# Norm weights at the split, weight work behind the norm chain, one more kept unit, and a skip term on TensorE, in a two-layer trunk kernel

## The chip, the cores and the metric

The kernel runs on one core of a Trainium2 chip. The metric is the device time of one execution in microseconds (us), lower is better. Three timed runs of the kernel before took 2191.85, 2193.81 and 2197.32 us; their median is 2193.81 us. A separate, profiled execution gives the trace.

The engines are named as in the profile: PE is TensorE's matmul, PEld its weight load, DVE is VectorE, ACT is ScalarE, POOL is GpSimd, and SP issues the DMAs from one queue, in order.

## The reference, cut to what matters

One sequence of 256 tokens, width 2048, goes through two layers. Layer 0 mixes with a diagonal state-space model (S5) and a gated linear unit (GLU), layer 1 with latent attention. Each is followed by a gated feed-forward part (FFN) with a short causal convolution. Around every part stand two RMS norms with their own weights: one on what the part puts out, one on what the next part reads.

```python
for l in range(DEPTH):                      # 2 layers
    h = rmsnorm(x, norm_g[l, 0])
    m = s5_mixer(h, ...) if l == 0 else mla_mixer(h, ..., *shared_kv(x, kv_norm_g, ...))
    x = x + rmsnorm(m, norm_g[l, 1])        # weight gpost
    h = rmsnorm(x, norm_g[l, 2])            # weight gpre of the FFN
    f = conv_ffn(h, ...)                    # (gelu(conv(h @ w_gate)) * (h @ w_up)) @ w_down
    x = x + rmsnorm(f, norm_g[l, 3])
# rmsnorm(x, g) = x * rsqrt(mean(x*x) + 1e-6) * g
# in s5_mixer: y = einsum(h_re, c_re) - einsum(h_im, c_im) + d_skip * u
```

All of it is float32. `d_skip * u` is the skip term.

## The kernel before, in words

**Split products.** A float32 product is made of three matmuls (`mm3`, L108 to L110) on a high and a low part of each operand. `split` (L73, L74) makes the parts: ScalarE copies the source into a rounded high part, VectorE subtracts that from the source. `wunit` (L77) loads a unit of weights, 1 MB, into one of two buffers called `raw` and splits it in two halves; each half costs one ScalarE and one VectorE instruction on 128x1024. The parts go into rotating buffers (`whi`, `wlo`, three each) or, with `slots=`, into places of their own where they can stay (tiles named `x` in the profile).

**Tokens in two blocks.** The 256 tokens are two blocks of 128 (`tb` 0 and 1). Activations for the next part are kept transposed and split, in four tiles `act`.

**Stages.** S5 in 16 rounds of 8 channel groups (on all engines, with early GLU units put in between), the rest of the GLU, FFN of layer 0, attention, FFN of layer 1. In the FFN, 21 of the 22 pairs of weight columns use activations of both blocks as the moving operand (`inner`, L114 and L115).

**The turn between two parts** is what the change is about; there are three: GLU to FFN, FFN to attention, attention to FFN. Each goes like this.

1. The last weight units of a part are *kept* (`held`): block 0 is multiplied as each arrives (5 units in the GLU by `HOLD5` and `LATE`, 4 in attention's output projection by `HOLD`), and the matmuls of block 1 on the same units come after that. They are TensorE's work while block 0 goes through its norms.
2. `finish_chunk` (L163 to L166) takes the sum of squares of each 512 columns on ScalarE (L139) and multiplies by `gpost` on VectorE (L166). In the GLU, `finish` (L629 to L632) comes before it: two bias additions, a sigmoid on ScalarE, a product.
3. `post_norm` (L168): `rstd1` (L141 to L153) adds the sums (`tot`, L145), GpSimd takes a power (`rs_y`, L147), three tiny VectorE instructions refine it (L149, L151, L153). Then for each of the four chunks, L172 adds the normed output to `x`, ScalarE takes the squares of the new `x` (L139), and, where the next part is an FFN, L178 multiplies `x` by `gpre` into `f`.
4. `pre_scale` (L180): a second `rstd1`, and L182 scales the identity matrix by it. Call the instruction d0 for block 0 and d1 for block 1.
5. `pre_turn` (L185 to L192): 16 matmuls (32 records in the profile) with d0 or d1 as the moving operand transpose and scale a block at once (L191); each bank of four is split into `act`.
6. The next part's first weight units are kept too: four units, multiplied for block 0 (`swapped`, L708, in the FFN; `down` in attention), then block 1's `pre_turn` (that is `tail()`), then block 1's products.

So d0 is what TensorE waits for after the kept units, and d1 is what it waits for after block 0's products on the next four.

**What sets the order.** Each engine works through its instructions in one fixed order. A scheduler makes that order when the program is built, by priority and by a model of when operands are ready. It therefore puts splits of the next part's weights between the steps of the norm chain wherever the model has them ready.

**S5.** `part_k` sums products of small tiles in PSUM (`tiled`, L399), ScalarE copies 112 of 128 columns of each group into `K` (L451), VectorE adds the skip term `dB` to the last 16 while copying them (L452), and 128 records of small matmuls read `K` (L467).

**Other loads.** `gkv` and `gq` are the first DMAs of the program (L604, L605), ahead of S5's own; the `gpre` and `gpost` rows are broadcast to all partitions, 1 MB each (`gain_load`, L134).

Of the kernel before, what the change touches and what calls it, by code (L numbers as in the profile page):

```python
# [35 lines left out]
HOLD5 = ((0, 2), (4, 6), (10, 12), (8, None), (None, None))  # L36
LATE = ((1, 1), (2, 1), (3, 1), (2, 0), (3, 0))
# [7 lines left out]
def tile_trunk(ctx: ExitStack, tc: tile.TileContext, a: dict):  # L45
# [84 lines left out]
    def gain_tile(src):  # L130
        return T(env["ap"], [P, D], F32, "gb", 2), src
# [31 lines left out]
    def finish_chunk(f, fst, tb, n, g):  # L163
        c = f[tb][:, n * 512 : (n + 1) * 512]
        sq_acc(c, fst[tb][:, n : n + 1])
        dve.tensor_tensor(c, c, g[0][:, n * 512 : (n + 1) * 512], op=ALU.mult)  # L166

    def post_norm(f, fst, tb, x, xst, g):  # L168
        r = rstd1(fst[tb], D)
        for n in range(NCH):  # L170
# [6 lines left out]
            if g is not None:  # L177
                dve.tensor_tensor(f[tb][:, c], x[tb][:, c], g[0][:, c], op=ALU.mult)  # L178

    def pre_scale(xst):  # L180
        d = T(env["ap"], [P, 512], F32, "xh", 2)[:, :P]
        dve.tensor_scalar(d, ident, rstd1(xst, D), None, op0=ALU.mult)  # L182
        return d

    def pre_turn(h, d, tb):  # L185
        for n in range(NCH):
# [5 lines left out]
            split(*acts4(tb, n, slice(0, 4)), ptv)  # L192
# [50 lines left out]
    def glu_early(f, n, b, half):  # L243
        hv = glu_load(n, b, half)
        banks = [accb(), accb()]
        for tb in range(NB):
            hk, u = hv
            for i, (wh, wl) in enumerate(u):
                for k in range(hk):
                    j = i * hk + k  # L250
                    mm3(banks[tb], *acts(tb, 4 * b + j), wh[:, k, :], wl[:, k, :], j == 0, j == 3)
        o = half * 1024 + n * 512
# [8 lines left out]
    def s5(f):  # L261
        with tc.tile_pool(name="s5", bufs=2) as q1:
            w0 = env["wp"]
            dt = T(q1, [P, P], F32, "dt", 1)
            sync.dma_start(dt, a["sL"].partition_broadcast(P))
            sA = T(q1, [P, 2, P], F32, "sA", 1)
            sync.dma_start(sA, a["sA"])
            sync.dma_start(cst, a["cst"])
# [6 lines left out]
            sync.dma_start(dB, a["dX"])  # L275

# [117 lines left out]
            def tiled(*terms):  # L394
                o = wk()[:, : NG * P]
                for g in range(NG):
                    for i, (lhs, rhs) in enumerate(terms):
                        for j in range(4):
                            pe.matmul(  # L399
                                o[32 * j : 32 * j + 32, g * P : (g + 1) * P], lhs(g, j), rhs(g, j),  # L400
                                start=g == 0 and i == 0, stop=g == NG - 1 and i == len(terms) - 1,
                                tile_position=(0, 32 * j),
                            )
                return o
# [33 lines left out]
            def part_k(sb, e1, ff):  # L438
# [7 lines left out]
                def e67(g, j):  # L446
                    return flat2(e1[:, 4 * g + j, 6:8, :])

                pkg = by_group(tiled(*((e67, lambda g, j, z=z: flat2(z[:, 4 * g + j, 1:9, :])) for z in ff)))
                K = Ks[sb % 2]  # L450
                act.activation(K[:, :, :112], pkg[:, :, :112], AF.Copy)  # L451
                dve.tensor_tensor(  # L452
                    K[:, :, 112:128],
                    pkg[:, :, 112:128],
                    dB.rearrange("p (g q) -> p g q", q=16)[:, NG * sb : NG * (sb + 1), :],
                    op=ALU.add,
                )
# [360 lines left out]
    def attention(tail, gains, f, fst, done):  # L818
        with tc.tile_pool(name="at", bufs=2) as q1:
# [200 lines left out]
            for g in gains:  # L1020
                gain_load(g)
# [157 lines left out]
```

## Time and profile before

| what | us |
|---|---|
| timed runs, median (lowest to highest) | 2193.81 (2191.85 to 2197.32) |
| the profiled execution | 2187.58 |
| its span, first to last instruction | 2185.8 |
| PE busy in the span | 2079.0 (95%) |
| VectorE busy | 1408.8 (64%) |
| ScalarE busy | 1122.4 (51%) |
| GpSimd busy | 19.8 (1%) |

The profiled execution is one run; the 1.78 us between its time and its span lie around the first and the last instruction. Rows of a timeline read: start, duration, engine, line of the kernel, operation, out<-in with the shapes, count, and in brackets how long the engine had stood still before it and what ended that. Rows of the table of windows read: window, its length, then for PE, PEld, DVE, ACT and POOL the busy us and in brackets the instructions, then TensorE's granted clock as a share of full speed, the DMA engines' busy share, and GB/s. A busy time of an instruction includes some overlap with its neighbour: instructions that follow each other directly start a little sooner than the durations say.

### The profile page before, as it was taken

How to read it: one execution, taken by the hardware profiler on the slowest of the kernel's cores; microseconds unless marked ns; L12 is line 12 of the kernel's file. 1: busy time of each engine (PE TensorE's matmuls, PEld its weight loads, DVE VectorE, ACT ScalarE, POOL GpSimd, SP SyncE). 2: the span in 40 equal slices, each digit the busy share in tenths (PEclk: the TensorE clock that was granted, in tenths of full speed). 3: DMA queues.
4: the chain of work that ended last, by engine and by line, in shares of the span. 5: the costliest groups of instructions: out<-in, count | busy, mean ns of one | idle time of the engine just before them, and what ended most of it. 6: DMA issues, size and time to landing. Idle time of an engine off the chain costs nothing.

```text
span 2185.8 us, 32404 instructions
## 1 busy us (share of the span) xinstructions
PE 2079.0 (95%) x13268; PEld 1764.2 (81%) x13268; DVE 1408.8 (64%) x1940; ACT 1122.4 (51%) x1695; POOL 19.8 (1%) x57
## 2 busy tenths in 40 slices
PE   3788999899999999999989999989999999999998
PEld 2566777888888888888878998788888888888886
DVE  7999666666466556655686665566646655665567
ACT  6677445455455445544464554545545544554444
POOL 0000000000000000000000000000000000000000
PEclk9999999999999999999999999999999999999999
DMA  4132476455565555555564434635555555555654
GB/s 131 50 98 75 154 233 206 145 188 179 193 197 187 193 193 191 178 190 193 192 200 129 136 118 155 212 123 189 189 193 193 180 187 193 193 183 184 194 191 154
DMA packets 280966, 374.74 MB, mean 171 GB/s; under 512 B 9200, under 2 KB 196208, under 8 KB 279792
## 3 DMA queue, kind: packets, MB, share of 16 engines
q1 hardware_dynamic: 280816, 372.66, 52.4%
q8 instruction: 104, 1.70, 0.3%
q14 instruction: 46, 0.38, 0.1%
HBM read 370.54 MB, written 2.10 MB: 170 GB/s over the span
## 4 chain that ended last, share of the span: by engine, by line
PE 82%; DVE 10%; DMA 4%; ACT 3%; issue 1%; POOL 0%; SPq 0%; DVEq 0%; POOLq 0%; ACTq 0%
PE wk L114 29%; PE wk L115 15%; PE acc L108 9%; PE acc L109 9%; PE acc L110 9%; DMA raw<-in_w_glu 3%; PE wk L108 2%; PE wk L109 2%; PE wk L110 2%; DVE wlo L74 2%; PE acc L191 1%; DVE x L74 1%; ACT whi L73 1%; DVE f L431 1%; DVE f L430 1%
## 5 line engine op out<-in xcount | busy, mean ns | idle before, releaser
L74 DVE TENSOR_TENSOR wlo<-raw,whi 128x1024 fp32r<-128x1024 f32 (+2 forms) x640 | 761.0, 1191 | 584.0 <-ACT whi L73 579.3
L73 ACT ACTIVATE whi<-raw 128x1024 fp32r<-128x1024 f32 (+2 forms) x640 | 658.3, 1031 | 635.3 <-PE wk L114 245.6
L114 PE MATMUL wk<-act,whi 128*128 128x512 f32 x2688 | 941.9, 395 | 0.0
L115 PE MATMUL wk<-act,wlo 128*128 128x256 f32 x2688 | 753.0, 280 | 0.0
L114 PEld LDWEIGHTS wk<-act,whi 128*128 128x128 f32 x2688 | 504.1, 188 | 119.3
L115 PEld LDWEIGHTS wk<-act,wlo 128*128 128x128 f32 x2688 | 507.4, 189 | 0.3
L108 PE MATMUL acc<-whi,hh 128*128 128x512 f32 x652 | 255.4, 392 | 0.0
L109 PE MATMUL acc<-wlo,hh 128*128 128x512 f32 x652 | 255.3, 392 | 0.0
L110 PE MATMUL acc<-whi,hl 128*128 128x512 f32 x652 | 254.3, 391 | 0.0
L108 PEld LDWEIGHTS acc<-whi,hh 128*128 128x128 f32 x652 | 122.4, 188 | 27.2 <-ACT hh L73 0.5
L109 PEld LDWEIGHTS acc<-wlo,hh 128*128 128x128 f32 x652 | 122.4, 188 | 27.0 <-DVE wlo L74 0.5
L110 PEld LDWEIGHTS acc<-whi,hl 128*128 128x128 f32 x652 | 122.4, 188 | 26.9
L108 PE MATMUL acc<-whi,act 128*128 128x512 f32 (+1 forms) x332 | 126.4, 381 | 2.7 <-ACT act L73 2.7
L109 PE MATMUL acc<-wlo,act 128*128 128x512 f32 (+1 forms) x332 | 124.9, 377 | 1.9 <-DVE wlo L74 1.9
L110 PE MATMUL acc<-whi,act 128*128 128x512 f32 (+1 forms) x332 | 124.3, 375 | 0.1
L765 DVE SCALAR_TENSOR_TENSOR cv<-gs,cw,cv 128x255 f32<-128x255 f32 (+1 forms) x168 | 77.2, 480 | 3.0
L109 PEld LDWEIGHTS acc<-wlo,act 128*128 128x128 f32 x332 | 62.5, 188 | 14.9 <-DVE wlo L74 4.0
L108 PEld LDWEIGHTS acc<-whi,act 128*128 128x128 f32 x332 | 62.5, 188 | 14.5 <-ACT act L73 3.0
L110 PEld LDWEIGHTS acc<-whi,act 128*128 128x128 f32 x332 | 62.5, 188 | 11.5 <-DVE act L74 0.5
L763 ACT ACTIVATE cv<-gs,cb,cw 128x256 f32<-128x256 f32 x84 | 50.5, 601 | 36.5 <-DVE gs L715 36.5
L714 ACT ACTIVATE us<-wk 128x256 f32<-128x256 f32 x84 | 31.7, 380 | 60.3 <-PE wk L115 60.3
L714 ACT ACTIVATE gs<-wk 128x256 f32<-128x256 f32 x84 | 32.0, 381 | 59.8 <-PE wk L115 59.8
(282 smaller groups left out, 2342.5 us busy)
## 6 DMA issues: line engine op xcount, KB each, us to landing
raw<-in_w_gate SPq DMA_DIRECT2D x88, 1024.0 KB, 5.0
raw<-in_w_up SPq DMA_DIRECT2D x88, 1024.0 KB, 4.9
raw<-in_w_down SPq DMA_DIRECT2D x88, 1024.0 KB, 4.9
raw<-in_w_glu SPq DMA_DIRECT2D x32, 1024.0 KB, 6.2
raw<-in_w_o SPq DMA_DIRECT2D x16, 1024.0 KB, 4.9
raw<-in_w_ukv SPq DMA_DIRECT2D x8, 1024.0 KB, 5.3
gb<-in_norm_g SPq DMA_DIRECT2D x6, 1024.0 KB, 6.7
raw<-in_w_uq SPq DMA_DIRECT2D x8, 768.0 KB, 4.4
```

The lines of the kernel that those rows point to most:

```text
L73: act.activation(hi, src, AF.Copy)
L74: (eng or dve).tensor_tensor(lo, src, hi.bitcast(F32), op=ALU.subtract)
L108: pe.matmul(o, lh, rh, start=first, stop=False)
L109: pe.matmul(o, lh, rl, start=False, stop=False)
L110: pe.matmul(o, ll, rh, start=False, stop=last)
L114: pe.matmul(ov, lh, r, start=first, stop=False)
L115: pe.matmul(ov[:, 0, :], ll, r[:, 0, :], start=False, stop=last)
L191: pe.matmul(ptv[:, k, :], h[:, o : o + P], d, start=True, stop=True)
L430: dve.tensor_tensor(f1, zt(0, 0, 9, 1), bc(2, 9), op=ALU.mult)
L714: act.activation(z[:, ft, :], two[ft][:, S:], AF.Copy)
L763: act.activation(cv[:, ft, :], gv[:, ft, :], AF.Identity, scale=cw[:, 2, n : n + 1], bias=cb[:, n : n + 1])
L765: dve.scalar_tensor_tensor(cv[:, ft, sh:], gv[:, ft, : S - sh], cw[:, 2 - sh, n : n + 1], cv[:, ft, sh:], op0=ALU.mult, op1=ALU.add,)
```

## The change

Five edits are made together.

- **Norm weights at the split.** `gpre` is no longer multiplied into `f` (L178 goes, with the 1 MB broadcast of the weights). It is loaded as a column per 128 channels (`gf`), and `pre_turn` applies it while splitting: per bank four ScalarE and four VectorE instructions on 128x128 with a scale pointer, where one of each on 128x512 stood.
- **Weight work behind the norm chain.** d0 is remembered (`env["turn"]`). `tc.issue_after(d0)` orders the VectorE instructions of a block of code behind d0 on VectorE. It is put around the splits of the next part's kept units (in the FFN all but the first, in attention the third and fourth), around block 1's `finish` in the GLU, and around block 1's `gpost` product elsewhere. It orders no instruction of another engine.
- **One more kept unit.** Six instead of five in the GLU; in the output projection the last unit of the third chunk of columns is kept as well, and block 1's part of that chunk moves behind block 0's end. One `gb` buffer goes.
- **Skip term on TensorE.** Four small matmuls with the identity (columns of 32) add `dB` to the PSUM bank; ScalarE copies all 128 columns, and L452 goes.
- **Order of the first loads.** `sA` comes first, then `dt`; `gkv`, `gq` and the new `gf` come behind S5's loads.

```diff
-HOLD5 = ((0, 2), (4, 6), (10, 12), (8, None), (None, None))
-LATE = ((1, 1), (2, 1), (3, 1), (2, 0), (3, 0))
+HOLD6 = ((0, 2), (4, 6), (10, 12), (14, 16), (8, None), (None, None))
+LATE = ((1, 1), (2, 1), (3, 1), (1, 0), (2, 0), (3, 0))
...
-        return T(env["ap"], [P, D], F32, "gb", 2), src
+        return T(env["ap"], [P, D], F32, "gb", 1), src
...
     def finish_chunk(f, fst, tb, n, g):
         c = f[tb][:, n * 512 : (n + 1) * 512]
         sq_acc(c, fst[tb][:, n : n + 1])
-        dve.tensor_tensor(c, c, g[0][:, n * 512 : (n + 1) * 512], op=ALU.mult)
+        with behind(env["turn"] if tb else None):
+            dve.tensor_tensor(c, c, g[0][:, n * 512 : (n + 1) * 512], op=ALU.mult)
...
             sq_acc(x[tb][:, c], xst[:, n : n + 1])
-            if g is not None:
-                dve.tensor_tensor(f[tb][:, c], x[tb][:, c], g[0][:, c], op=ALU.mult)
...
+    def behind(ins):
+        return nullcontext() if ins is None else tc.issue_after(ins)
+
-            split(*acts4(tb, n, slice(0, 4)), ptv)
+            hi, lo = acts4(tb, n, slice(0, 4))
+            if g is None:
+                split(hi, lo, ptv)
+                continue
+            for k in range(4):
+                gk = g[:, 4 * n + k : 4 * n + k + 1]
+                act.activation(hi[:, k, :], ptv[:, k, :], AF.Copy, scale=gk)
+                dve.scalar_tensor_tensor(
+                    lo[:, k, :], ptv[:, k, :], gk, hi[:, k, :].bitcast(F32), op0=ALU.mult, op1=ALU.subtract
+                )
...
-            sync.dma_start(dt, a["sL"].partition_broadcast(P))
             sA = T(q1, [P, 2, P], F32, "sA", 1)
             sync.dma_start(sA, a["sA"])
+            sync.dma_start(dt, a["sL"].partition_broadcast(P))
...
+            for z, v in ((gkv, a["gkv"]), (gq, a["gq"]), (gf[0], a["gf"][0]), (gf[1], a["gf"][1])):
+                sync.dma_start(z, v)
...
+                if diag is not None:
+                    for j in range(4):
+                        pe.matmul(
+                            by_group(o)[32 * j : 32 * j + 32, :, 112:128], ident[:, 32 * j : 32 * j + 32], diag,
+                            start=False, stop=True, tile_position=(0, 32 * j),
+                        )
...
-                act.activation(K[:, :, :112], pkg[:, :, :112], AF.Copy)
-                dve.tensor_tensor(
-                    K[:, :, 112:128],
-                    pkg[:, :, 112:128],
-                    dB.rearrange("p (g q) -> p g q", q=16)[:, NG * sb : NG * (sb + 1), :],
-                    op=ALU.add,
-                )
+                act.activation(K[:, :, :P], pkg, AF.Copy)
...
-                    if n == 3 and (b, half) > (1, 0):
+                    if n == 3 and (b, half) > (0, 1):
...
-                    gain_load(gains[1])
...
-            finish(3, tb, banks, bb)
+            with behind(env["turn"] if tb else None):
+                finish(3, tb, banks, bb)
...
-                                held.append((which, kh, wunit(v, 8, S, slots=HOLD[len(held)])))
+                                with behind(before if held else None):
+                                    held.append((which, kh, wunit(v, 8, S, slots=HOLD[len(held)])))
...
+                    with behind(before if which == 0 and un > 1 else None):
+                        hv = wunit(
...
-                    if n < NCH - 1:
+                    if n == NCH - 2 and un == 3:
+                        late = (load(n, un, (10, 12)), banks)
+                        down(banks[0], un, 0, late[0])
+                        chunk(n, 0, banks)
+                    elif n < NCH - 1:
                         project(n, un, banks)
...
-                for tb in range(NB):
-                    if tb:
+                for tb in range(NB if n == NCH - 2 else 0, NB):
+                    if tb and held:
+                        down(late[1][1], 3, 1, late[0])
+                        chunk(NCH - 2, 1, late[1])
                         for un, hv in enumerate(held):
                             down(banks[1], un, 1, hv)
...
-                    dg[tb] = pre_scale(xst[tb])
+                    dg[tb], ins = pre_scale(xst[tb])
+                    if tb == 0:
+                        env["turn"] = ins
             elif not last:
-                pre_turn((x if gn is None else f)[tb], dg[tb], tb)
+                pre_turn(x[tb], dg[tb], tb, gpre)
```

More of the change, by code (lines that the diff above doesn't have):

```diff
@@ L1 @@
 import math
-from contextlib import ExitStack
+from contextlib import ExitStack, nullcontext
 import concourse.bass as bass
@@ L251, in glu_early, with glu_keep @@
                     mm3(banks[tb], *acts(tb, 4 * b + j), wh[:, k, :], wl[:, k, :], j == 0, j == 3)
+        glu_keep(f, n, b, half, banks)
+    def glu_keep(f, n, b, half, banks):
         o = half * 1024 + n * 512
@@ L603, in tile_trunk @@
     gkv, gq = T(cp, [P, KT], F32, "gkv"), T(cp, [P, KT], F32, "gq")
-    sync.dma_start(gkv, a["gkv"])
-    sync.dma_start(gq, a["gq"])
+    gf = [T(cp, [P, KT], F32, f"gf{l}") for l in range(2)]
     krE, krO = T(cp, [P, S], F32, "krE"), T(cp, [P, S], F32, "krO")
@@ L622, in rope_tables, with glu_rest @@
         sincos(rsin, rcos, rr, rn, cst[:, C_RS : C_RS + 1])
-    def glu_rest(q1, todo, f, fst, gains, done):
+    def glu_rest(q1, todo, f, fst, gain, done):
         def finish(n, tb, banks, bb):
@@ L632, in finish @@
             dve.tensor_tensor(c, c, sg, op=ALU.mult)
-            finish_chunk(f, fst, tb, n, gains[0])
+            finish_chunk(f, fst, tb, n, gain)
         def bias(n):
@@ L660, in glu_rest @@
                     if b == 0:
-                        gain_load(gains[0])
+                        gain_load(gain)
                     bb = bias(b)
@@ L678, in glu_rest, with ffn @@
                 done(0, 1)
-            finish(3, tb, banks, bb)
+            with behind(env["turn"] if tb else None):
+                finish(3, tb, banks, bb)
             done(tb, 0)
         return lambda: done(1, 1)
-    def ffn(l, tail, gains, f, fst, done):
+    def ffn(l, tail, before, gain, f, fst, done):
         with tc.tile_pool(name=f"ff{l}", bufs=2) as q1:
@@ L775, in ffn @@
                 if part == len(PARTS) - 2:
-                    for g in gains:
-                        if g is not None:
-                            gain_load(g)
+                    gain_load(gain)
                 def load(n, un, slots=(None, None)):
@@ L790, in evac @@
                     if last:
-                        finish_chunk(f, fst, tb, n, gains[0])
+                        finish_chunk(f, fst, tb, n, gain)
                 if last:
@@ L815, in ffn, with attention @@
         return lambda: done(1, 1)
-    def attention(tail, gains, f, fst, done):
+    def attention(tail, before, gpost, f, fst, done):
         with tc.tile_pool(name="at", bufs=2) as q1:
@@ L1018, in attention, with chunk @@
                     q = {"kv": kv, "qn": qn, "qr": rope(q1, qs_, br[:, S:])}
-            for g in gains:
-                gain_load(g)
+            gain_load(gpost)
+            env["yp"] = q1
+            def chunk(n, tb, banks):
+                c = f[tb][:, n * 512 : (n + 1) * 512]
+                act.activation(c, banks[tb], AF.Copy)
+                finish_chunk(f, fst, tb, n, gpost)
             for n in range(NCH):
@@ L1030, in attention @@
                         down(banks[0], un, 0, held[un])
-                for tb in range(NB):
-                    if tb:
+                for tb in range(NB if n == NCH - 2 else 0, NB):
+                    if tb and held:
+                        down(late[1][1], 3, 1, late[0])
+                        chunk(NCH - 2, 1, late[1])
                         for un, hv in enumerate(held):
                             down(banks[1], un, 1, hv)
-                        if held:
-                            done(0, 1)
-                    c = f[tb][:, n * 512 : (n + 1) * 512]
-                    act.activation(c, banks[tb], AF.Copy)
-                    finish_chunk(f, fst, tb, n, gains[0])
+                        done(0, 1)
+                    chunk(n, tb, banks)
                     if held:
@@ L1146, in _arrays @@
         "b_glu": g("ssm_b_glu"),
+        "gf": np.stack([pn(g("norm_g")[l, 2]) for l in range(2)]),
         "gkv": pn(g("kv_norm_g")),
```

43 lines of the change are left out of this document (23 added, 20 removed).

## The prediction, made before the changed kernel was run

> **What bounds the kernel now.** I read the page first, then the table of windows, then the timelines of single engines around the places where TensorE stands still.
>
> ```profile
> span 2185.8 us, 32404 instructions
> PE 2079.0 (95%) x13268; PEld 1764.2 (81%) x13268; DVE 1408.8 (64%) x1940; ACT 1122.4 (51%) x1695; POOL 19.8 (1%) x57
> ...
> 50.00:200.00 150.00, 123.21 (x2157) 91.54 (x2142) 144.09 (x234) 104.69 (x208) 0.43 (x6) 0.99 0.25 73
> 340.00:372.00 32.00, 30.90 (x129) 23.52 (x128) 18.42 (x18) 16.16 (x20) 0.00 (x0) 1.00 0.69 204
> 1460.00:2165.00 705.00, 704.99 (x3716) 602.53 (x3715) 426.02 (x500) 346.89 (x441) 0.00 (x0) 1.00 0.57 188
> ```
>
> The last row is the second FFN: TensorE never stops, and nothing in the change touches its matmuls. The kernel can win only in the 107 us in which TensorE is idle: in S5, where VectorE is the bound (144.09 of 150), in the GLU, and at the turns. TensorE's timeline shows the three turns, and a warm `pre_turn` to compare with:
>
> ```profile
> 393.24 6.28 PE L191 MATMUL acc<-xh,f 128*128 128x128 f32 x32 [7.29 <-DVE xh L182]
> 410.76 3.73 PE L191 MATMUL acc<-xh,f 128*128 128x128 f32 x32
> 1145.34 5.72 PE L191 MATMUL acc<-xh,x 128*128 128x128 f32 x32 [5.92 <-DVE xh L182]
> 1428.87 5.61 PE L191 MATMUL acc<-xh,f 128*128 128x128 f32 x32 [7.41 <-DVE xh L182]
> ...
> 389.00:390.00 1.00, 0.00 (x0) 0.00 (x0) 1.00 (x3) 1.00 (x2) 0.67 (x1) 0.50 0.00 0
> 301.00:302.00 1.00, 1.00 (x3) 0.75 (x3) 0.16 (x1) 0.00 (x0) 0.00 (x0) 0.50 0.82 215
> ```
>
> At each turn TensorE waits 5.9 to 7.4 us for d0 (L182), and the 32 records after it take 5.6 to 6.3 us where the warm ones take 3.73: in the stall the granted clock falls to 0.50. The two FFN turns thus cost at most 7.29 + 2.55 and 7.41 + 1.88, 19.1 us together.
>
> **What the change does to the first turn.** VectorE's timeline from block 0's last bias (L631) to d0, and to d1, with the windows and groups of that stretch:
>
> ```profile
> 375.60 0.69 DVE L631 TENSOR_TENSOR f<-acc,bias 128x512 f32<-128x512 f32 x1 [1.75 <-PE acc L110]
> 380.18 1.23 DVE L74 TENSOR_TENSOR x<-raw,x 128x1024 fp32r<-128x1024 f32 x1 [0.22 <-ACT x L73]
> 392.30 0.69 DVE L166 TENSOR_TENSOR f<-f,gb 128x512 f32<-128x512 f32 x1
> 392.90 0.28 DVE L182 TENSOR_SCALAR xh<-cst,rs_r 128x128 f32<-128x128 f32 x1
> 405.39 0.29 DVE L182 TENSOR_SCALAR xh<-cst,rs_r 128x128 f32<-128x128 f32 x1
> ...
> 375.60:393.18 17.58, 10.35 (x45) 8.07 (x43) 17.29 (x32) 11.97 (x21) 2.04 (x3) 0.86 0.54 178
> 393.18:405.68 12.50, 12.44 (x86) 12.44 (x87) 11.31 (x24) 4.95 (x12) 2.08 (x4) 0.79 0.78 264
> ...
> L74 DVE TENSOR_TENSOR x<-raw,x 128x1024 fp32r<-128x1024 f32 x5 | 6.0, 1220 | 0.2 <-ACT x L73 0.2
> L74 DVE TENSOR_TENSOR wlo<-raw,whi 128x1024 fp32r<-128x1024 f32 x3 | 3.6, 1219 | 0.0
> L178 DVE TENSOR_TENSOR f<-x,gb 128x512 f32<-128x512 f32 x8 | 5.2, 685 | 0.0
> ```
>
> VectorE is full, 17.29 of 17.58 us, before d0. Eight weight splits stand in the two windows. Four of them, of the second and third kept unit, stand ahead of d0, the one at 380.18 the first, and will be ordered behind it: 4 x 1.14 (durations less the overlap of about 0.08) = 4.6 us. Block 1's four `finish` instructions (one like 392.30 each) go behind it: 4 x 0.6 = 2.4. The four L178 of block 0 vanish: 2.4. That is 9.4 us, and leaves 7.9 us of work. But the full engine hid the chain's other waits: two GpSimd powers, and the last ScalarE squares behind the last L172.
>
> ```profile
> 380.04 0.55 POOL L147 TENSOR_TENSOR rs_y<-tot,cst 128x1 f32<-128x1 f32 x1 [273.01 <-DVE tot L145]
> 389.33 1.45 POOL L147 TENSOR_TENSOR rs_y<-tot,cst 128x1 f32<-128x1 f32 x1 [8.70 <-DVE tot L145]
> ```
>
> I put these at 3.5 us: two powers near 0.55 to 1.45 plus hand-overs, and about 1.3 us for the last squares, with one ScalarE weight copy of the third unit still in between, since only VectorE is ordered. So d0 starts at 375.6 + 7.9 + 3.5 = 387.0, 5.9 us earlier. The kept matmuls end at 393.24 - 7.29 = 385.95. The sixth unit adds 12 matmuls of 30.90/129 = 0.24 us behind block 0's end, 2.9 us at most; but TensorE is already 97% busy there (row 340 to 372), so most of this is work only moved among itself, and I count 1 us. The gap left is 0.3 us (0 to 2).
>
> [...]
>
> **What is late next: d1.** Behind d0 now stand the six splits of units two to four, block 1's finish and norm chain, and block 0's splits with the weight in them. The nearest rows for the short instructions are of S5:
>
> ```profile
> 21.29 2.45 ACT L347 ACTIVATE act<-raw,rs_r 128x128 f32<-128x128 f32 x8
> 8.07 0.29 DVE L220 SCALAR_TENSOR_TENSOR R<-w,e 128x128 f32<-128x128 f32 x1
> ```
>
> On VectorE four times 0.25 (0.29 less overlap, plus a little for the pointer) replace 0.6 per bank: +1.6 us per block. On ScalarE four times 2.45/8 = 0.31 replace 0.5: +2.9 us per block, beside `pre_turn` and the first `swapped` products, which need a further bank only every 1.4 us (a bank serves half a unit, an eighth of the 11.3 us from 399.5 to 410.76): I cost it at nothing; without that cover it is 0.7 us for the first bank. VectorE's whole work from L631 to d1 changes by -4.8 (eight L178) + 1.6, and gains the 3.5 us of exposed waits: d1 stays near 405.4 + 0.3 = 405.7. Before, d1 had 5 us to spare, as TensorE came to block 1's `pre_turn` only at 410.76. Now TensorE would come there at 387.3 + 3.7 + 11.3 = 402.3 and wait for d1. So the turn gains 410.8 - 405.7 = 5.1 us, not 9.8. Ends: 8.5 if the splits fill the chain's holes well and d1 is in time; 2 if the fourth unit is late, whose load cannot be issued until the second unit's split frees its `raw` buffer, now behind d0; SP's later loads queue behind that one, and the first FFN products wait for it.
>
> **The third turn** is the same without `finish`:
>
> ```profile
> 1422.88 2.35 DVE L74 TENSOR_TENSOR x<-raw,x 128x1024 fp32r<-128x1024 f32 x2
> 1428.53 0.28 DVE L182 TENSOR_SCALAR xh<-cst,rs_r 128x128 f32<-128x128 f32 x1
> 1439.63 0.29 DVE L182 TENSOR_SCALAR xh<-cst,rs_r 128x128 f32<-128x128 f32 x1
> ...
> 1415.90:1428.81 12.91, 5.57 (x25) 4.22 (x23) 12.27 (x26) 7.67 (x15) 3.34 (x5) 0.88 0.48 158
> 1428.81:1439.92 11.11, 11.05 (x80) 11.05 (x81) 10.90 (x22) 6.39 (x14) 1.51 (x4) 0.83 0.59 220
> ```
>
> Ahead of d0 go four splits (two at 1422.88), four L178 and one L166: 7.6 of 12.3 us; with 3.5 us exposed d0 comes at 1424.1, 4.4 us earlier. TensorE ran dry at 1421.46; with 1 us of cover the gap is 1.7 us. The row at 301 us, behind gaps of 0.86 and 0.76 us, shows that even this can halve the clock for about 3 us, so I add 0.8. `pre_turn` then ends at 1428.6 and block 0's products at 1439.9. d1: 1439.6 - 4.8 + 1.6 + 0.6 (the moved chunk's L166) + 3.0 = 1440.0. So 1440.3 against 1445.75: 5.4 us (2 to 8.5). [...]
>
> **The second turn** loses only block 1's products with `gpost` ahead of d0; its third and fourth unit stand behind d0 already.
>
> ```profile
> L166 DVE TENSOR_TENSOR f<-f,gb 128x512 f32<-128x512 f32 x2 | 1.4, 688 | 0.1
> ```
>
> Two such between 1143.5 and d0: 1.2 us less, gap 4.7. I take 1.0 (0 to 1.2).
>
> **S5, start and GLU.**
>
> ```profile
> L452 DVE TENSOR_TENSOR K<-wk,dB 128x32 f32<-128x32 f32 x16 | 2.9, 182 | 2.5 <-ACT K L451 2.5
> 32.66 1.94 PE L399 MATMUL wk<-f,e 128*32 128x128 f32 x32 [8.18 <-DVE e L435]
> ...
> 0.74 0.38 SPq L604 DMA_DIRECT2D gkv<-in_gkv  x1
> 2.11 0.43 SPq L267 DMA_DIRECT2D sA<-in_sA  x1
> 5.50 0.43 DVE L300 TENSOR_TENSOR pu<-sA 128x256 f32<-128x256 f32 x1 [5.50 <-DMA sA<-in_sA]
> ...
> 285.85 0.50 SPq L134 DMA_DIRECT2D gb<-in_norm_g  x1
> 298.88 0.50 PE L109 MATMUL wk<-wlo,act 128*128 128x512 f32 x1 [0.76 <-DVE wlo L74]
> ```
>
> L452 frees VectorE of 16 x 0.12 and of 2.5 us of waiting, 4.4 us at best. In its place come eight matmul records a round, at 1.94/32 = 0.06 each 0.5 us, or 7.8 us in 16 rounds if all lay on the path; TensorE has 27 us of room in the 150. I take +1.0 (-5 to +4.4). At the start VectorE waits for `sA`, which moves to the head of the queue, 1.37 us earlier; `dt` and the inputs gain 0.9: 1.0 (0.5 to 1.4). The four small loads now queue ahead of the rounds' own; at 0.4 us an issue they delay those by some 0.8 us net, which S5's range covers. The broadcast at 285.85 goes: 1 MB less where the loads set the pace, just before two gaps and the halved clock at 301: 1.5 (0 to 3).
>
> Sum: 5.1 + 5.4 + 1.0 + 1.0 + 1.0 + 1.5 = 15.0 us. The profiled execution, 2187.58, would go to 2172.6. It lies 6.2 us below the median of the runs; against the median I forecast 2193.8 - 15.0 = 2178.8 us.
>
> **Rivals.**
> - *d1 is in time.* VectorE's holes are filled, and both FFN turns give 8.5; with the ends of the rest (1.2, 4.4, 1.4, 3) the gain is 27: 2167. For: VectorE is idle 3.5 us longer in the chain and could split there if the scheduler's order allowed it; against: the edges forbid just that.
> - *The wait moves.* The fourth unit's load or the first splits stall `swapped`, or ScalarE's unordered weight copies hold the squares back, or the scheduler put other VectorE work into the opening: the turns give 2 each, the rest 2: gain 6, 2188. For: SP stands in order behind the `raw` buffer; against: 8.5 us pass before the fourth unit is used.
> - *Slower: the identity matmuls do not overlap.* If each of the eight records runs alone for about 0.28 us, a round gets 2.2 us longer between ScalarE's copy and L467, 36 us in all; less 14 elsewhere and 4.4 on VectorE that makes 2211. It decides from 1.6 us a round. Against: the same column tiles run at 0.06 in the row at 32.66, and TensorE has room.
> - *The edges bind nothing* (the order was nearly so already): then the L178 and the loads alone remain, about 7: 2187. The row at 380.18 speaks against it.
>
> **How the numbers follow.** Forecast 0.56, d1 in time 0.13, the wait moves 0.18, slower 0.06, edges bind nothing 0.07. A measurement of this kernel can tell about 0.3%, 6.6 us. Faster by more than that are the first two (0.69), a third of the moved wait (0.06) and under half of the last (0.03): 0.78; slower is the identity matmuls' 0.06; the rest, 0.16, is the same. The range runs from the first rival, 2167, to the second, 2188, and some 3 us beyond each for the spread of the runs: 2164 to 2191.
>
> **What would show it.** Right: no L178, no L452; d0 some 6 and 4 us earlier after block 0's end, gaps before L191 under 2.5 us at the FFN turns, its 32 records near 3.7 us, and TensorE waiting for d1 before block 1's `pre_turn`. Wrong: gaps of 5 us at L191, a wait in `swapped` for L74 of the fourth unit, or longer rounds in S5.

## The result, and the profile after

The changed kernel took 2181.03 us (median of 4 runs, 2179.92 to 2182.69) against 2194.05 us for the kernel before (4 runs, 2191.85 to 2197.32): ratio 0.9942, 95% interval 0.9928 to 0.9956. A second measurement, among the experiments below, gave 2184.90 against 2193.22 us, ratio 0.9962 (0.9950 to 0.9974). So the change is worth 8 to 13 us; 15.0 were predicted, and 2178.8 us in a range of 2164 to 2191. The profiled execution took 2181.60 us, 6 us less than that of before, which was an unusually quick one.

The page, two lines:

```profile
span 2179.8 us, 32719 instructions
PE 2084.0 (96%) x13396; PEld 1765.9 (81%) x13396; DVE 1405.5 (64%) x1956; ACT 1135.1 (52%) x1743; POOL 18.5 (1%) x57
```

TensorE's timeline at the three turns (`pre_turn` is now L193; L108 is the first product of `swapped`):

```profile
388.20 3.84 PE L193 MATMUL acc<-xh,x 128*128 128x128 f32 x32
394.09 0.39 PE L108 MATMUL acc<-x,act 128*128 128x256 f32 x1 [2.05 <-DVE act L201]
407.22 3.84 PE L193 MATMUL acc<-xh,x 128*128 128x128 f32 x32 [1.46 <-DVE xh L181]
...
1142.69 5.87 PE L193 MATMUL acc<-xh,x 128*128 128x128 f32 x32 [4.77 <-DVE xh L181]
...
1419.46 3.84 PE L193 MATMUL acc<-xh,x 128*128 128x128 f32 x32 [0.91 <-DVE xh L181]
1424.83 0.38 PE L108 MATMUL acc<-x,act 128*128 128x256 f32 x1 [1.53 <-DVE act L201]
1438.31 3.84 PE L193 MATMUL acc<-xh,x 128*128 128x128 f32 x32 [1.77 <-DVE xh L181]
```

The long waits for d0 at the FFN turns are gone, and with them the half clock behind them: 3.84 us for the 32 records at a granted clock of 1.00, where 6.28 and 5.61 stood at a mean of 0.59 and 0.67. Two new waits are there at each FFN turn in this trace: one for short splits of `act` (L201) before `swapped` can start, which I call the gap at the first bank, and one for d1 before block 1's `pre_turn`. The name is short for more than it says: in both traces of this kernel, and at both FFN turns, TensorE goes on about 0.05 us after the end of the seventh of the sixteen short splits, though a bank has four. Why it is the seventh isn't shown. VectorE's timeline, with d0 and d1 (L181), and GpSimd's:

```profile
377.38 0.69 DVE L650 TENSOR_TENSOR f<-acc,bias 128x512 f32<-128x512 f32 x1 [1.75 <-PE acc L110]
386.59 0.16 DVE L145 TENSOR_REDUCE tot<-st 128x1 f32<-128x5 f32 x1 [1.13 <-ACT junk L139]
387.86 0.29 DVE L181 TENSOR_SCALAR xh<-cst,rs_r 128x128 f32<-128x128 f32 x1
406.88 0.29 DVE L181 TENSOR_SCALAR xh<-cst,rs_r 128x128 f32<-128x128 f32 x1
```

```profile
386.83 0.54 POOL L147 TENSOR_TENSOR rs_y<-tot,cst 128x1 f32<-128x1 f32 x1 [4.55 <-DVE tot L145]
396.86 1.45 POOL L147 TENSOR_TENSOR rs_y<-tot,cst 128x1 f32<-128x1 f32 x1 [9.48 <-DVE tot L145]
```

d0 comes 10.5 us after block 0's last bias addition, where 17.3 stood; the wait for the last squares (1.13 us) has come to light, as predicted.

For the experiments I use two stretches of the trace. A holds the first FFN turn: it runs from block 0's last bias addition to block 1's `pre_turn` at turn 1 (407.22 - 377.38 here). B holds the third turn, but all of attention with it: it runs from block 1's `pre_turn` at turn 2 to the same place at turn 3. Its first ends, in before and in the changed kernel (the rows break off before the last of the 32 records):

```profile
1161.98 2.62 PE L191 MATMUL acc<-xh,x 128*128 128x128 f32 x22
```

```profile
1159.52 2.84 PE L193 MATMUL acc<-xh,x 128*128 128x128 f32 x24
```

Each A and B in the table is from one trace.

| kernel | A, us | B, us | time, us | ratio to before (95%) |
|---|---|---|---|---|
| before; again | 35.2; 34.7 | 283.8; 284.8 | 2194.05; 2196.02 | 1; 0.9999 |
| changed; again | 29.8; 30.0 | 278.8; 280.2 | 2181.03; 2184.90 | 0.9942; 0.9962 |
| order alone | 36.1 | 282.9 | 2192.76 | 0.9990 (0.9980 to 1.0001) |
| changed, no order | 35.0 | 282.1 | 2192.92 | 0.9990 (0.9979 to 1.0002) |
| changed, weights in `f` | 34.3 | 280.5 | 2192.42 | 0.9995 (0.9983 to 1.0007) |
| changed, no kept unit | 30.3 | 282.3 | 2185.54 | 0.9963 (0.9949 to 0.9977) |
| changed, plain split | 30.7 | 277.1 | 2181.54 | 0.9943 (0.9929 to 0.9957) |
| changed, later units | 29.8 | 279.6 | 2183.26 | 0.9951 (0.9937 to 0.9965) |
| changed, skip on VectorE | 29.8 | 278.9 | 2181.89 | 0.9941 (0.9927 to 0.9954) |

The changed kernel itself differs by 4 us between its two measurements, so differences of less than that between rows are read from the traces, not from the times. Two traces of one kernel differ by up to 0.4 us in A and 1.5 us in B.

### The profile page after: what moved, and what is told of

The parts are those of the page before. It is cut to its first block, busy times and chain, and to the rows that moved or that the text cites. A ratio compares the mean times of both kernels' runs of the same rounds, so it can differ in the third digit from the quotient of the medians.

```text
span 2179.8 us, 32719 instructions
## 1 busy us (share of the span) xinstructions
PE 2084.0 (96%) x13396; PEld 1765.9 (81%) x13396; DVE 1405.5 (64%) x1956; ACT 1135.1 (52%) x1743; POOL 18.5 (1%) x57
## 3 DMA queue, kind: packets, MB, share of 16 engines
q8 instruction: 105, 1.72, 0.3%
## 4 chain that ended last, share of the span: by engine, by line
PE 80%; DVE 9%; DMA 5%; ACT 4%; issue 1%; POOL 0%; SPq 0%; DVEq 0%; POOLq 0%; ACTq 0%
PE wk L114 28%; PE wk L115 14%; PE acc L108 9%; PE acc L109 9%; PE acc L110 9%; DMA raw<-in_w_glu 3%; PE wk L109 2%; PE wk L108 2%; PE wk L110 2%; DVE wlo L74 2%; ACT whi L73 1%; DVE x L74 1%; DMA raw<-in_w_o 1%; ACT junk L139 1%; DVE f L452 1%
## 5 line engine op out<-in xcount | busy, mean ns | idle before, releaser
L74 DVE TENSOR_TENSOR wlo<-raw,whi 128x1024 fp32r<-128x1024 f32 (+1 forms) x636 | 755.8, 1190 | 576.6 <-ACT whi L73 573.7
L73 ACT ACTIVATE whi<-raw 128x1024 fp32r<-128x1024 f32 (+1 forms) x636 | 653.9, 1031 | 631.2 <-PE wk L114 246.7
L108 PE MATMUL acc<-whi,hh 128*128 128x512 f32 x652 | 255.5, 392 | 0.0
L108 PEld LDWEIGHTS acc<-whi,hh 128*128 128x128 f32 x652 | 122.4, 188 | 27.2 <-ACT hh L73 0.5
L110 PEld LDWEIGHTS acc<-whi,hl 128*128 128x128 f32 x652 | 122.4, 188 | 27.0
L109 PEld LDWEIGHTS acc<-wlo,hh 128*128 128x128 f32 x652 | 122.4, 188 | 26.9 <-DVE wlo L74 0.6
L108 PE MATMUL acc<-whi,act 128*128 128x512 f32 (+1 forms) x316 | 120.7, 382 | 1.3 <-ACT whi L73 1.0
L109 PE MATMUL acc<-wlo,act 128*128 128x512 f32 (+1 forms) x316 | 119.2, 378 | 2.4 <-DVE wlo L74 2.4
L110 PE MATMUL acc<-whi,act 128*128 128x512 f32 (+1 forms) x316 | 118.3, 375 | 0.0
L108 PEld LDWEIGHTS acc<-whi,act 128*128 128x128 f32 x316 | 59.8, 189 | 12.6 <-ACT whi L73 1.4
L110 PEld LDWEIGHTS acc<-whi,act 128*128 128x128 f32 x316 | 59.8, 189 | 10.8 <-issue 0.4
```

Of the source, the lines that this page charges most:

```text
L73: act.activation(hi, src, AF.Copy)
L74: (eng or dve).tensor_tensor(lo, src, hi.bitcast(F32), op=ALU.subtract)
L108: pe.matmul(o, lh, rh, start=first, stop=False)
L109: pe.matmul(o, lh, rl, start=False, stop=False)
L110: pe.matmul(o, ll, rh, start=False, stop=last)
```

## The experiments

**Theory:** at the FFN turns VectorE's queue sets the time; the order brings d0 forward, and something else must keep d1 and the fourth unit from coming too late. **Rivals:** the removal of L178 does it alone; the kept unit does it; or much of the gain lies in S5 and the loads, since the first two traces differ by only 6 us and the times by 13.

### Both kernels once more

No edit.

> The kernel before, once more, for a second trace of it: its profiled execution came 6 us below the median of its timed runs, so a trace may not stand for those. Every theory: ratio 1.000 to the kernel before (0.9985 to 1.0015). If the theory of the turns is right (all of the 13 us comes from the three turns, none from S5 or the loads), the new trace should show the end of S5 (last record of tiled) near 259 us, 5 us later than in the changed kernel by chance of the run alone, or the turns must show more than the first trace did. If the rest of the 13 us is a lasting loss in S5 of the kernel before (rival), the end of S5 lies near 259 us in this trace and again in those of kernels that put the skip term back on VectorE.

> The changed kernel once more, beside three variants of it on the same chip, and for a second trace. Every theory: ratio to before 0.9942 (0.9928 to 0.9956). Theory (the turns hold some 10.5 of the 13 us): from block 0's last bias to block 1's pre_turn again 29.8 us, against 35.2 and 34.7 in two traces of before, and from the second to the third turn's end 278.8 against 283.8 and 284.8; the end of S5 may lie anywhere from 253 to 258.

Measured: before again 2196.02 us, ratio 0.9999 (0.9989 to 1.0008); changed again as above. The rows are S5's window in before, in before again and in the changed kernel; the number after the bracket of POOL is the granted clock:

```profile
35.00:255.00 220.00, 184.60 (x3058) 138.26 (x3057) 197.41 (x316) 145.82 (x284) 0.43 (x6) 0.98 0.26 77
```

```profile
35.00:255.00 220.00, 184.51 (x2986) 138.36 (x2985) 193.81 (x311) 142.85 (x279) 0.43 (x6) 0.94 0.25 76
```

```profile
35.00:255.00 220.00, 188.98 (x3168) 142.17 (x3167) 194.72 (x299) 146.94 (x282) 0.43 (x6) 0.95 0.26 74
```

The same kernel ended S5 at 253.3 and at 259.2 us, with a clock of 0.98 and 0.94. So the first trace of before had 6 us of luck in S5 beside the second, and that is most of the gap between traces and times. The two traces of the changed kernel end S5 at 254.5 and 255.5. From means of two, A shrinks by 5.0 and B by 4.8 us: 9.8 of the 8 to 13. The other stretches change less, and not all for the better: up to the last bias addition the changed kernel is 1.9 us ahead, from A to B it takes 0.6 us longer (752.3 and 753.4 against 751.2 and 753.3) and behind B 1.2 us longer (741.5 and 741.6 against 740.1 and 740.6). No run explains the last; the prediction expected no change there. In the second trace of the changed kernel there is no wait for d1 at turn 1: a half clock behind the gap at the first bank (0.50 from 394 to 397 us) made TensorE come to block 1's `pre_turn` only at 406.53, about when d1 ended (GpSimd's last power ahead of it started at 405.16, 0.70 us sooner than in the first trace), and A is the same.

### The order alone, and all but the order

```diff
# order alone: before, plus
+with behind(env["turn"] if tb else None): ...   # finish, gpost
+with behind(before if held else None): ...      # kept units
# no order: changed, with
-        return nullcontext() if ins is None else tc.issue_after(ins)
+        return nullcontext()
```

> Before plus the ordering alone: the splits of the next kept units, and block 1's finish and gpost products, behind d0; L178 stays, no kept unit more. Theory (VectorE's order at the turn is what saves): d0 comes about 3.5 us earlier at turn 1 and 3 us earlier at turn 3 (7 us of work leave, 3.5 us of waits come to light), but with L178 still in place d1 comes 3 us later than before, near 408.5, so that TensorE waits there and keeps only 2 us a turn: 4 us in all, ratio 0.998 (0.996 to 0.9995). Rival (the removal of L178 is what saves, not the order): ratio 1.000 or above it. Rival (the kept unit): 1.000.

> The changed kernel with no ordering behind d0, all else as it is. Theory: the splits and block 1's finish stand ahead of d0 again; the gap before block 0's pre_turn is back at 3 to 5 us at both FFN turns and its 32 records at 5.5 us, while d1 is in time: 6 to 9 us slower than the changed kernel, 2187 to 2190, ratio to before 0.997. Rival (L178's removal and the kept unit do it): gap under 2 us, time 2181 to 2183, ratio 0.994 to 0.995.

Either part alone is worth 1 to 2 us, with intervals that reach no gain at all; both together are worth 8 to 13. TensorE at turn 1 in the kernel with the order alone (L195 is its `pre_turn`):

```profile
393.74 5.47 PE L195 MATMUL acc<-xh,f 128*128 128x128 f32 x32 [2.42 <-DVE xh L186]
408.98 0.38 PE L108 MATMUL acc<-whi,act 128*128 128x256 f32 x1 [1.24 <-ACT whi L73]
411.99 0.58 PE L109 MATMUL acc<-wlo,act 128*128 128x256 f32 x1 [2.63 <-DVE wlo L74]
```

and the changed kernel without it, both FFN turns:

```profile
397.47 5.89 PE L193 MATMUL acc<-xh,x 128*128 128x128 f32 x32 [6.41 <-DVE xh L181]
1432.45 5.47 PE L193 MATMUL acc<-xh,x 128*128 128x128 f32 x32 [4.40 <-DVE xh L181]
```

Without the order the old wait for d0 is back, though L178 is gone: the rival of L178 alone falls. With the order alone the wait for d0 shrinks from 7.29 to 2.42 us, and the gain is given back 15 to 18 us later. I had expected that wait at d1. It stands at the fourth unit instead (`whi`, `wlo`), 3.9 us: the rival that the prediction called "the wait moves".

### Which part is the partner

```diff
# weights in f: changed, with L178, its broadcast and the plain split of before
+                dve.tensor_tensor(f[tb][:, c], x[tb][:, c], g[0][:, c], op=ALU.mult)
-                pre_turn(x[tb], dg[tb], tb, gpre)
+                pre_turn((x if gn is None else f)[tb], dg[tb], tb, None)
# no kept unit: changed, with HOLD of five units and the old output projection
-                    if n == 3 and (b, half) > (0, 1):
+                    if n == 3 and (b, half) > (1, 0):
```

> The changed kernel with gpre multiplied into f on VectorE as before (L178 and the broadcast back, plain split in pre_turn); ordering, kept units, skip term and load order stay. Theory A (L178's removal is the partner of the ordering): d0 2.4 us later, and d1 3 us later than in the changed kernel, so TensorE waits some 5 us before block 1's pre_turn: 6 to 11 us slower than the changed kernel at the two FFN turns together, 2187 to 2192, ratio 0.997 to 0.9995. Theory B (the kept unit is the partner): within 3 us of the changed kernel, 2180 to 2184, ratio 0.994 to 0.995.

> The changed kernel without the additional kept unit (five units in the GLU, and the third chunk of the output projection not kept). So far the ordering alone gave 1.3 us, all else without the ordering 1.1 us, both together 13. Theory A (order and VectorE's load together: the ordering makes d0 early, the removal of L178 keeps d1 from coming too late, each is worth little without the other): the kept unit is worth what the prediction put, 1 us a turn, part of it absorbed by the wait for d1 behind it; 1 to 4 us slower than the changed kernel, 2182 to 2185, ratio 0.995 to 0.996; gap before block 0's pre_turn 1 to 3 us. Theory B (the kept unit is the partner that the ordering needs): 8 to 12 us slower, 2189 to 2193, gaps over 4 us and half-clock stretches behind them.

With the weights back in `f` nothing measurable is left (0.9995). TensorE and VectorE of that kernel, turn 1 (L179 is its product with gpre):

```profile
391.41 3.84 PE L195 MATMUL acc<-xh,f 128*128 128x128 f32 x32 [1.82 <-DVE xh L183]
405.02 0.38 PE L108 MATMUL acc<-whi,act 128*128 128x256 f32 x1 [1.25 <-ACT whi L73]
408.04 0.58 PE L109 MATMUL acc<-wlo,act 128*128 128x256 f32 x1 [2.63 <-DVE wlo L74]
```

```profile
405.56 1.29 DVE L179 TENSOR_TENSOR f<-x,gb 128x512 f32<-128x512 f32 x2
406.76 1.22 DVE L74 TENSOR_TENSOR wlo<-raw,whi 128x1024 fp32r<-128x1024 f32 x1
```

The low part of the fourth unit stands on VectorE behind block 1's products with gpre, and TensorE waits for it: the same 2.63 us as with the order alone. So theory A holds in the time, with the fourth unit in place of d1 at turn 1. Two things stay open. The first of the two waits (1.25 us, for ScalarE's copy) is the load's: it was issued at 398.37, behind the second unit's split, and ScalarE could copy it only at 403.93, against 393.01 and 398.23 in the changed kernel. So part of the loss comes through the `raw` buffer, and the order alone with a third such buffer was not tried. And at turn 3 little of the loss is seen: B is 280.5 us, 1.0 more than in the changed kernel and within chance, so A and B together hold 5.4 us of a difference of 7 to 11 by the times. The kept unit is a smaller matter, but more than the 1 us a turn that the prediction gave it, at turn 3:

```profile
1423.33 5.46 PE L193 MATMUL acc<-xh,x 128*128 128x128 f32 x32 [3.63 <-DVE xh L181]
```

Without it the gap is 2.7 us longer than the 0.91 above and the 32 records 1.6 us longer, 4.3 in all; at turn 1 the gap is only 0.60 in place of none. By A and B it is worth 0.4 and about 3 us, since part of it is taken up by the wait for d1 behind it. The times, 2185.54 against 2181.03 and 2184.90 us, don't decide it.

### The short splits, and a later place for the units

```diff
# plain split: changed, with (this kernel leaves out the weights gpre)
-            if g is None:
+            if True:
# later units: the second unit's first half behind the last x update, the rest behind the first bank
-                                with behind(before if held else None):
+                                when = ((None, None), (before[1], before[2]), (before[2],) * 2, (before[2],) * 2)[len(held)]
```

> The changed kernel with a plain split in pre_turn, one ScalarE and one VectorE instruction per bank in place of four and four; it leaves out the weights gpre altogether. It prices the short instructions of the norm weights at the split, which the prediction costed at 1.6 us of VectorE per block and nothing for TensorE. Theory A (VectorE sets d1, and d1 sets the turn): the wait for d1 (1.46 and 1.77 us in the changed kernel) goes and the gap behind the first bank (2.05 and 1.53) shortens to about 1: 3 to 5 us faster than the changed kernel, 2176 to 2178, ratio 0.992. Rival (the gap comes from the order of VectorE's queue and not from the size of the splits): the gaps stay, under 1.5 us faster, 2180 to 2181.

> The changed kernel with another order at the FFN turns: the first half of the second kept unit is split behind block 0's last update of x (in the 1.1 us in which VectorE waits for the last squares), the other kept units behind the last short split of block 0's first bank, not behind d0; finish, the gpost product and attention's units stay behind d0. Theory (in the changed kernel the gap of 2.05 and 1.53 us behind the first records of swapped is VectorE's splits of weights standing between the short splits of that bank): the gap falls under 0.7 us at both turns, d1 comes up to 1 us earlier; 1 to 4 us faster than the changed kernel, 2177 to 2180. Rival (the weights are needed as early as they come; to hold them back only moves the wait to L74 of the second or third unit): same gap sum, 2180 to 2183.

The theory fell both times. With the plain split, the gap behind the first bank does fall, to 0.23 us, and B gains some 2 us; but turn 1 becomes 0.8 us longer, and the time stays:

```profile
392.04 0.39 PE L108 MATMUL acc<-x,act 128*128 128x256 f32 x1 [0.23 <-DVE act L74]
407.66 4.61 PE L193 MATMUL acc<-xh,x 128*128 128x128 f32 x20 [3.83 <-issue]
```

The profile names no releaser for the 3.83 us; d1 ended 0.1 us before that `pre_turn`, at 407.56. VectorE had work to spare ahead of d1, but stood still, and ScalarE's row names the cause:

```profile
399.55 1.23 DVE L74 TENSOR_TENSOR wlo<-raw,whi 128x1024 fp32r<-128x1024 f32 x1 [2.17 <-ACT whi L73]
```

```profile
398.46 2.01 ACT L73 ACTIVATE whi<-raw 128x1024 fp32r<-128x1024 f32 x2 [3.26 <-DMA raw<-in_w_up]
```

It is the load of the fourth unit, which has to wait for a `raw` buffer. In the changed kernel ScalarE waits 1.11 us for it in the same place. With later units the gaps at turn 1 only change places, 1.72 us at the first bank and 1.21 at the fourth unit in place of 2.05 and 1.46:

```profile
395.57 0.39 PE L109 MATMUL acc<-x,act 128*128 128x256 f32 x1 [1.72 <-DVE act L205]
404.70 0.38 PE L109 MATMUL acc<-whi,act 128*128 128x256 f32 x1 [0.33 <-ACT whi L73]
405.96 0.39 PE L110 MATMUL acc<-wlo,act 128*128 128x256 f32 x1 [0.88 <-DVE wlo L74]
```

No weight split stands between the short splits here, and the gap is 1.72 us all the same: TensorE goes on behind the eighth of them, with block 1's `gpost` product in between. So weight splits alone don't make that gap.

### The skip term

```diff
# skip on VectorE: changed, with L452 of before in place of the identity matmuls
# identity four times: changed, with dB scaled by 0.25 and
+                    for again in range(4):
```

> The changed kernel with the skip term added on VectorE as before, no identity matmuls. Theory (the skip edit saves nothing): within 2 us of the changed kernel, 2179 to 2183, ratio to before 0.993 to 0.995. Rival (the part of the 13 us that the traces do not show at the turns comes from S5): 5 to 7 us slower than the changed kernel, 2186 to 2188, ratio 0.997. The prediction's step, a gain of 1.0 us, is inside the theory's bounds.

> The changed kernel with the four identity matmuls of each round of S5 issued four times, on a quarter of the skip term, so that the sum is the same: 24 records more in each of 16 rounds. Theory (they run overlapped, at about 0.04 us each, in TensorE time that S5 has to spare): 24 x 0.04 x 16 = 15 us of TensorE time, of which at most a third shows: 0 to 5 us slower than the changed kernel, 2181 to 2186. Rival (each record stands on the path between ScalarE's copy and the matmuls behind it): 15 us and more, 2196 or above.

On VectorE again the kernel took 2181.89 us, ratio 0.9941: the edit is worth nothing that can be measured, though the 1.0 us that was forecast lies within the intervals too. S5 ended at 254.9 us there, so the skip term on VectorE isn't a lasting loss in S5 either. With four times the matmuls it took 2184.76 us, ratio 0.9964 (0.9951 to 0.9976), against 0.9962 for the changed kernel on the same chip: again nothing. The groups of the identity matmuls, in the changed kernel and with four times as many:

```profile
L422 PE MATMUL wk<-dB,cst 128*32 128x32 f32 x128 | 4.5, 201 | 0.0
```

```profile
L424 PE MATMUL wk<-dB,cst 128*32 128x32 f32 x512 | 8.1, 200 | 0.0
```

384 records more cost 3.6 us of TensorE's time, not the 15 that I expected, and S5 has the room: TensorE was busy 188.98 of the 220 us of its window in the changed kernel. The prediction's slower rival, 36 us, falls with its price: 0.035 us a record in the changed kernel, not 0.28.

### A third raw buffer, and GpSimd

```diff
# third raw: changed, with (and so in the two other places that make a `raw`)
-        raw = T(wp, [P, nk, cols], F32, "raw")
+        raw = T(wp, [P, nk, cols], F32, "raw", 3)
# fourth on GpSimd: that, and the low parts of the FFN's fourth kept unit on GpSimd
+                                    onp = (None,) if len(held) == 3 else ()
```

> The changed kernel with three raw buffers in place of two, so that the load of the fourth kept unit needn't wait for the second unit's split, which now stands behind d0 (its load went out at 393.0, and ScalarE waited 1.1 us for it). Theory A (VectorE's own work between d0 and d1, 16.6 us without a hole, sets d1; the load is in time): the load goes out near 385, d1 stays within 0.5 us, time within 2 us of the changed kernel. Theory B (the load holds up ScalarE and so VectorE's queue): d1 comes 1 to 2 us earlier at both FFN turns, 2 to 4 us faster than the changed kernel, 2177 to 2179.

> As the kernel with three raw buffers, and the low parts of the FFN's fourth kept unit are made on GpSimd, which is idle there, in place of VectorE: two instructions of 128x1024 less, 2.3 us, between d0 and d1. Theory A (VectorE's work sets d1): d1 comes up to 2.3 us earlier at both FFN turns, 2 to 4 us faster than the changed kernel, 2177 to 2179, if GpSimd needs under 4 us for each. Rival (GpSimd is much slower and slows VectorE beside it: its power on 128x1 took 1.45 us beside a split and 0.54 alone): TensorE waits for the fourth unit's low parts and block 1's power queues behind them, 3 us or more slower, 2184 or above.

With three raw buffers the kernel took **2162.99 us** (2160.60 to 2166.03), ratio 0.9863 (0.9846 to 0.9880): 22 us under the changed kernel measured beside it (18 under its first measurement), the fastest version of this study. Theory B named the buffer, but for the fourth unit at the FFN turns; its 2 to 4 us were far too small, because the larger part of the gain lies in the GLU, which neither theory looked at. The window behind S5, in the changed kernel and with three buffers:

```profile
255.00:340.00 85.00, 79.43 (x344) 62.92 (x343) 56.43 (x71) 39.74 (x49) 0.00 (x0) 1.00 0.75 234
```

```profile
255.00:340.00 85.00, 85.00 (x375) 69.82 (x374) 64.46 (x81) 47.52 (x60) 0.00 (x0) 1.00 0.79 249
```

TensorE no longer stops in this window of the GLU: 85.00 us busy in place of 79.43. In the changed kernel SP waits 56.5 us, from 255 to 345, for a split to free a buffer; with three buffers one load more is under way meanwhile. SP's rows, cut at 345 us, show the issues, and the first of the second row is one load further on. Over the same loads, from the fifteenth of the 32 to the last, an issue comes every 5.8 us with two buffers and every 5.1 with three:

```profile
299.80 43.20 SPq L79 DMA_DIRECT2D raw<-in_w_glu  x8
```

```profile
293.78 48.83 SPq L79 DMA_DIRECT2D raw<-in_w_glu  x11
```

Everything on VectorE and ScalarE then comes earlier, shown by the last bias addition, d0 and d1, and TensorE waits at one place in a turn:

```profile
359.27 0.69 DVE L650 TENSOR_TENSOR f<-acc,bias 128x512 f32<-128x512 f32 x1 [1.79 <-PE acc L110]
370.82 0.29 DVE L181 TENSOR_SCALAR xh<-cst,rs_r 128x128 f32<-128x128 f32 x1
390.65 0.29 DVE L181 TENSOR_SCALAR xh<-cst,rs_r 128x128 f32<-128x128 f32 x1
```

```profile
381.59 0.58 PE L108 MATMUL acc<-x,act 128*128 128x256 f32 x1 [2.07 <-DVE act L201]
1408.25 0.39 PE L108 MATMUL acc<-x,act 128*128 128x256 f32 x1 [3.07 <-DVE act L201]
```

d0 and d1 are 5 and 4 us ahead of the `pre_turn` that they serve (375.79 and 394.63), and at both FFN turns TensorE waits only at the first bank. By the traces some 10 us come from S5's end to block 1's `pre_turn`, 2 to 3 from turn 2, and 2 to 4 from B; 1 to 2 lie in S5 itself, where chance is as large. A itself is longer, 35.4 us: what is gained lies ahead of it. The changed kernel has one 8 KB `gb` buffer less per partition, and a raw buffer is as large; whether a third one would help the kernel before was not tried.

With the fourth unit's low parts on GpSimd as well it took 2168.58 us, ratio 0.9890 (0.9875 to 0.9905), 5.6 us more than without that. GpSimd's rows, VectorE beside them, and TensorE behind them:

```profile
378.71 5.47 POOL L74 TENSOR_TENSOR wlo<-raw,whi 128x1024 fp32r<-128x1024 f32 x2 [5.42 <-ACT whi L73]
```

```profile
379.83 2.13 DVE L651 TENSOR_TENSOR f<-f,sg 128x512 f32<-128x512 f32 x1
381.89 0.34 DVE L201 SCALAR_TENSOR_TENSOR act<-acc,gf,act 128x128 fp32r<-128x128 f32 x1
382.81 1.91 DVE L167 TENSOR_TENSOR f<-f,gb 128x512 f32<-128x512 f32 x1 [0.59 <-ACT junk L139]
```

```profile
386.86 0.58 PE L108 MATMUL acc<-x,act 128*128 128x256 f32 x1 [4.39 <-DVE act L201]
```

A split takes 2.7 to 2.8 us on GpSimd at this turn where VectorE takes 1.22, and two of VectorE's instructions beside it take 2.13 and 1.91 in place of 0.68; the gap at the first bank grows from 2.07 to 4.39 us. The rival was right in sign, set against the kernel with three buffers (its 2184 us started from the changed kernel's time), and wrong in the place of the wait.

## Why the prediction was right, and which of its terms were off

**The FFN turns** were predicted at 5.1 and 5.4 us and measured at 5.0 (A) and 4.8 (B, with attention in it). The limit was named rightly: d1, with TensorE waiting for it. d1 was forecast 30.1 us after the last bias addition (405.7 - 375.6) and came after 29.5. The single steps were less good. d0 came 0.9 us earlier after that addition than forecast; its second power, beside which no split stands any more, took 0.54 us where 1.45 stood. TensorE was to wait 3.4 us for d1 at turn 1 and waited 1.46 and, in the second trace, not at all, because it had lost time at the first bank. In the sum for the third turn d1 has 3.0 us of exposed waits where d0 has 3.5, without a reason; with 3.5 the forecast is 4.9.

**The first bank's split** was costed at nothing, and at 0.7 us without cover. TensorE waited 2.05 and 1.53 us there. It goes on behind the seventh short split and not the fourth, and a weight split and block 1's `finish` stand among them. That this did little harm to the total was luck: d1, behind it, was the later limit.

**The kept unit** was given 1 us a turn; at turn 3 its cover was worth 4.3 us (2.7 of gap and 1.6 of longer records), about 3 of it in B, at turn 1 less than 1.

**The second turn** gave what was predicted in the wait, which fell from 5.92 to 4.77 us, by 1.15, against 1.0 to 1.2. In the time it doesn't show: the stretch from A to B, which holds this turn, got 0.6 us longer.

**S5, start and GLU** were given 3.5 us, and the traces show 1.9 up to the last bias addition, less than the chance between two traces. Against 15.0 the spans of the traces differ by 9.9 us (means of two): 1.6 are missing here, 1.6 at the second turn, 1.2 behind B and 0.7 at the FFN turns. The skip term gave nothing measurable instead of 1.0. GLU's loads gave nothing that shows: from S5's end to the last bias addition the two traces of before took 122.4 and 122.9 us, those of the changed kernel 122.9 and 121.1. What the order of the first loads gave is open: S5 ended at 256.2 us before and at 255.0 after (means of two traces each), with a spread of 6 us within one kernel.

**Of the rivals**, "the edges bind nothing" fell with the run without the order, and the identity matmuls with the two runs on the skip term. "The wait moves" isn't the changed kernel's case, but it is that of both kernels that have the order and keep L178. The prediction counted the removal of L178 as 2.4 us ahead of d0 and as part of d1's account; that the order is worth next to nothing without it is what the prediction did not say. "d1 is in time" is the case with the third raw buffer, where d1 comes 4 us ahead of TensorE at turn 1. The prediction had named the fourth unit's wait for a `raw` buffer and thought it harmless, since 8.5 us pass before the unit is used; that two buffers also slow the GLU's loads it did not see.

## What to carry to other kernels

Moving work behind a critical chain pays only if the queue behind it has room: here the order alone and everything but the order were worth 1 to 2 us each and 8 to 13 together, so test such parts together and look for the next wait further on (15 us here), not only at the place that was mended. Where work is put off that frees a load buffer, the buffer is put off too; before reordering an engine's queue, ask whether one buffer more wouldn't help, which on top of this change was worth more than the change itself.

## What the runs showed of the hardware that I had not expected

**The clock after short gaps.** The gap of 2.05 us at the first bank stands in both traces of the changed kernel. These are the windows behind it, first in the second trace, then in the first:

```profile
394.00:395.00 1.00, 1.00 (x7) 1.00 (x7) 1.00 (x4) 0.84 (x4) 0.00 (x0) 0.50 1.06 376
395.00:396.00 1.00, 1.00 (x6) 1.00 (x6) 1.00 (x5) 0.26 (x2) 0.00 (x0) 0.50 1.05 360
```

```profile
394.00:395.00 1.00, 0.91 (x7) 0.91 (x8) 1.00 (x6) 0.84 (x4) 0.00 (x0) 1.00 0.80 162
```

The same gap was followed by half the clock in one execution and not in the other; the windows from 393 to 398 us of the second trace lost 1.7 us of full clock, which is about 3.4 us at one half. So behind a gap of some 2 us up to 1.7 us more was lost here, in one trace of two; what decides it isn't shown.

**GpSimd beside VectorE.** In the rows of the kernel with the fourth unit on GpSimd the two VectorE instructions that read two SBUF tiles (L651, L167) take 2.13 and 1.91 us where the changed kernel shows 0.68, three times as long, while L201, which reads PSUM, keeps its 0.34 us. L651 started at 379.83, 1.1 us after GpSimd's first split, and ended at 381.96; GpSimd's two splits ran from 378.71 to 384.18. The row names no wait, and what made it longer isn't shown. GpSimd's power on 128x1 took 1.45 us in the changed kernel at 396.86, started behind a weight split that ran from 396.70 to 397.91. In the kernel before, a power at 380.04 took 0.55 us and the split that started 0.14 us behind it its usual 1.23: there neither was longer than without the other.
